# Loading a weight block's high part by a converting DMA and summing its low part from DRAM, in one stretch of a hybrid attention, RG-LRU and S5 block

## The chip, the cores and the metric

One core of a Trainium2 chip runs the program. The metric is device time in microseconds, the median of three runs: 1568.6 us before (1568.36, 1568.6 and 1571.8). One more execution was profiled; the rows shown further down are from it.

## The reference, cut to what matters

Two layers work on 512 latent and 256 context tokens of width 1024 (768 columns in all). One input projection feeds three mixers: differential attention, a bidirectional RG-LRU, and an S5 state space with a gated linear unit. Each mixer's output is multiplied by a SiLU gate, projected (`w_branch`), weighted by a sigmoid gate, and the sum goes through `w_out`. Everything is float32.

```
def hybrid_layer(x, ctx, c, c_ctx, p, layer_idx, need_ctx):
    ...
    q_l, k_l, v_l, za_l, xr_l, zr_l, us_l, zs_l, gl_l = jnp.split(h_l @ p['w_in'], pts, axis=-1)
    ...
    yr_l, yr_c = rglru_branch(xr_l, xr_c, p['conv_w'], p['conv_b'], p['lru_wa'], p['lru_ba'],
                              p['lru_wx'], p['lru_bx'], p['lru_lam'])
    ys_l, ys_c = s5_branch(us_l, us_c, p['s5_lam_re'], p['s5_lam_im'], p['s5_log_dt'], p['s5_b_re'],
                           p['s5_b_im'], p['s5_c_re'], p['s5_c_im'], p['s5_d'], p['s5_w_glu'],
                           p['s5_b_glu'], need_ctx)
    x = x + gt_x[:, None] * gated_merge(ya_l, yr_l, ys_l, za_l, zr_l, zs_l, gl_l, p['w_branch'], p['w_out'])

def gated_merge(ya, yr, ys, za, zr, zs, gl, w_branch, w_out):
    y = jnp.stack([ya * jax.nn.silu(za), yr * jax.nn.silu(zr), ys * jax.nn.silu(zs)], axis=2)
    yb = jnp.einsum('btnw,nwd->btnd', y, w_branch)
    g = jax.nn.sigmoid(gl.reshape(*gl.shape[:2], N_BRANCH, D_MODEL))
    return jnp.sum(g * yb, axis=2) @ w_out
```

## The kernel before

A float32 product is made of three products in the faster format fp32r: activations and weights are each split in a high part, rounded to fp32r, and a low part, the rest; high x high, low x high and high x low are summed (`product`, L169). Weights come in blocks of 128 x 512 float32 (256 KB). A block is four tiles of 128 x 128; each is used for three passes over 512 and 256 columns, 24 matmuls in all.

`wsplit` (L154) prepares a block. SyncE (SP) loads it into a buffer `wr`; ScalarE (ACT) writes the high part `wh` (L162); the low part `wl` is `wr - wh`. Mostly VectorE (DVE) subtracts (L167). Where `by_dma` is set, ACT writes `wl = -wh` (L164) and GpSimd (POOL) issues a DMA that adds `wr` to `wl` (L165), with the sum made by the DMA. `wr`, `wh` and `wl` have three buffers each in the pool `ws`; the gate weights of the RG-LRU (`wlru`) have one each in a pool of their own.

`by_dma` is set in the first layer only, from `lru` to the end of the merge of S5's output, for 56 blocks in this order: for each of four RG-LRU tiles the gate weights `wlru`, two blocks of in-projection (`inproj`) for the tile and two for each of two merge gates (`gate`), with S5 steps between them; eight for the four output gates of the RG-LRU (`merge_y`); eight of its branch projection (`branch`, called w1 to w8 below); four of S5's gated linear unit (`wglu`, g1 to g4); eight for S5's output gates (z1 to z8). Beside the last twelve, `s5_tables` computes tables for layer 1 on DVE and POOL stores them in DRAM (`s5d<-tb`, L401). Attention follows, with `by_dma` off.

A scheduler puts each engine's instructions in order ahead of time; each engine then goes through its own queue in that order, and an instruction that waits holds up all behind it. Buffers are used in turn: a block's `wh` and `wl` can be written when the matmuls on the block three before are done.

Of the kernel before, what the change touches and what calls it, by code (L numbers as in the profile page):

```python
# [11 lines left out]
F32 = mybir.dt.float32  # L12
F32R = mybir.dt.float32r
AF = mybir.ActivationFunctionType
OP = mybir.AluOpType
# [36 lines left out]
def hybrid_kernel(ctx, tc, xT, cc, wmod, win, winv, wbr, wout, wglu, wlru, par, lqk, s5a, s5b, s5B, s5C, dsk, rope, outT):  # L52
    nc = tc.nc
    V, S, G, PE, SP = nc.vector, nc.scalar, nc.gpsimd, nc.tensor, nc.sync
# [30 lines left out]
    def f32(ap):  # L85
        return ap.bitcast(F32)
# [65 lines left out]
    by_dma = [False]  # L152

    def wsplit(src, n, p=None, bufs=3, keep=None):  # L154
        p = p or pW
        raw = p.tile([128, 512], F32, name="wr", tag="wr", bufs=bufs)
        if keep:
            p, bufs = keep, None
        wh = p.tile([128, 512], F32R, name="wh", tag="wh", bufs=bufs)
        wl = p.tile([128, 512], F32R, name="wl", tag="wl", bufs=bufs)  # L160
        SP.dma_start(raw, src)
        S.activation(wh, raw, AF.Copy)  # L162
        if by_dma[0]:
            S.activation(wl, f32(wh), AF.Copy, scale=-1.0)  # L164
            G.dma_start(wl, raw, accum_op=OP.add)  # L165
        else:
            V.tensor_sub(wl, raw, f32(wh))  # L167
        return wh.rearrange("p (k n) -> p k n", n=n), wl.rearrange("p (k n) -> p k n", n=n)

# [548 lines left out]
    for l in range(L):  # L718
# [12 lines left out]
        def us_w(b, p):  # L731
            return [wsplit(win[l, US_T + i, :, 4 * b:4 * b + 4, :].rearrange("p k n -> p (k n)"), 128, keep=p)
                    for i in range(3)]
# [37 lines left out]
        def inproj(ct, sg, dst=None):  # L771
            blocks = []
            for b in range(2):
                wh, wl = wsplit(win[l, ct, :, 4 * b:4 * b + 4, :].rearrange("p k n -> p (k n)"), 128)
                blocks.append((wh, wl, 4 * b, 4))
            out = (dst or acc)("ps_in") if len(sg) > 1 else narrow("ps_in")
            product(blocks, hr, sg, out)
            return out
# [30 lines left out]

        def lru(i):  # L810
            wh, wl = wsplit(wlru[l, i].rearrange("p a n -> p (a n)"), 128, pR, 1)
            po = inproj(XR_T + i, both)
            xp = pR.tile([128, TT + 6], F32, name="xp", tag="up")
# [161 lines left out]
        for n in range(4):  # L975
            wh, wl = wsplit(wglu[l, n].rearrange("p k n -> p (k n)"), 128)
# [87 lines left out]
        for h in range(4):  # L1064
# [5 lines left out]
            for q0 in ([0, 2, 4] if need else [0, 2]):  # L1070
# [5 lines left out]
                for qi in range(2):  # L1076
                    qt = q0 + qi
                    p = [pT.tile([128, TT], F32, name=f"p{c}", tag=f"p{c}", bufs=2 - c) for c in range(2)]
# [20 lines left out]
                    for k0 in range(0, nk, 4):  # L1099
# [5 lines left out]
                        src = pt[:, :(k1 - k0) * 128].rearrange("p (k q) -> p k q", q=128)  # L1105
# [94 lines left out]
        for dt in range(KT):  # L1200
            late = dt >= KT - LATE
            blocks = []
            for b in range(2):
                wh, wl = wsplit(wout[l, dt, :, 4 * b:4 * b + 4, :].rearrange("p k n -> p (k n)"), 128,
                                keep=pK if late else None)
# [139 lines left out]
```

## Time and profile before

| | us |
|---|---|
| median of three runs | 1568.6 |
| the profiled execution | 1571.89 |
| its span, first to last instruction | 1570.1 |
| TensorE busy in it | 1489.2 |
| mean granted TensorE clock | 0.982 of full speed |

The profiled execution is 3.3 us above the median of the runs, and 1.8 us longer than its span. A stretch of the trace is named by the microseconds from the span's start.

### The profile page before, as it was taken

How to read it: one execution, taken by the hardware profiler on the slowest of the kernel's cores; microseconds unless marked ns; L12 is line 12 of the kernel's file. 1: busy time of each engine (PE TensorE's matmuls, PEld its weight loads, DVE VectorE, ACT ScalarE, POOL GpSimd, SP SyncE). 2: the span in 40 equal slices, each digit the busy share in tenths (PEclk: the TensorE clock that was granted, in tenths of full speed). 3: DMA queues.
4: the chain of work that ended last, by engine and by line, in shares of the span. 5: the costliest groups of instructions: out<-in, count | busy, mean ns of one | idle time of the engine just before them, and what ended most of it. 6: DMA issues, size and time to landing. Idle time of an engine off the chain costs nothing. (4 is left out here: it accounts for less than half of the span.)

```text
span 1570.1 us, 24750 instructions
## 1 busy us (share of the span) xinstructions
PE 1489.2 (95%) x9096; PEld 1246.2 (79%) x9096; DVE 1125.0 (72%) x2312; ACT 818.7 (52%) x1468; POOL 172.2 (11%) x231
## 2 busy tenths in 40 slices
PE   4998899899999999999999999999999999999997
PEld 2786778788988888888778887777788988888777
DVE  6789899978367757658568863789775488397555
ACT  6676878664344534534325365666525365355433
POOL 1111111124000100000332310000000000000110
PEclk8998999999999999989999999999999999999999
DMA  8555444467311111115573762435454212111542
GB/s 279 167 151 119 112 110 105 89 158 197 94 52 43 42 53 46 49 34 177 193 250 125 258 201 82 143 111 162 118 168 132 81 61 58 65 61 54 174 148 94
DMA packets 111210, 189.13 MB, mean 120 GB/s; under 512 B 25328, under 2 KB 42352, under 8 KB 111088
## 3 DMA queue, kind: packets, MB, share of 16 engines
q1 hardware_dynamic: 97392, 158.17, 32.2%
q0 software_dynamic: 13696, 29.37, 8.1%
q8 instruction: 72, 1.18, 0.3%
q14 instruction: 50, 0.41, 0.1%
HBM read 145.02 MB, written 25.69 MB: 109 GB/s over the span
## 5 line engine op out<-in xcount | busy, mean ns | idle before, releaser
L162 ACT ACTIVATE wh<-wr 128x512 fp32r<-128x512 f32 x320 | 200.3, 629 | 367.2 <-PE ps_in L180 151.3
L180 PE MATMUL ps_in<-hH,wh 128*128 128x512 f32 x1248 | 376.5, 360 | 14.4 <-ACT wh L162 7.3
L180 PE MATMUL ps_in<-hH,wl 128*128 128x512 f32 x1248 | 378.6, 359 | 7.1 <-DMA wl<-wr 7.1
L180 PE MATMUL ps_in<-hL,wh 128*128 128x512 f32 x1248 | 375.5, 359 | 0.0
L167 DVE TENSOR_TENSOR wl<-wr,wh 128x512 fp32r<-128x512 f32 x264 | 187.5, 714 | 172.7 <-ACT wh L162 129.9
L180 PEld LDWEIGHTS ps_in<-hH,wh 128*128 128x128 f32 x1248 | 207.3, 192 | 52.3 <-ACT wh L162 8.4
L180 PEld LDWEIGHTS ps_in<-hH,wl 128*128 128x128 f32 x1248 | 207.7, 191 | 43.1 <-DMA wl<-wr 9.6
L180 PEld LDWEIGHTS ps_in<-hL,wh 128*128 128x128 f32 x1248 | 206.9, 191 | 31.8
L911 POOL TENSOR_TENSOR m<-m,g 128x768 f32<-128x768 f32 (+1 forms) x16 | 29.0, 1811 | 730.7 <-issue 348.4
L1091 ACT ACTIVATE p<-ps_s,mx 128x768 f32<-128x768 f32 (+1 forms) x80 | 65.2, 815 | 71.4 <-DVE mx L1090 67.5
L180 PE MATMUL ps_b<-yH,wh 128*128 128x512 f32 (+1 forms) x288 | 89.5, 359 | 0.6 <-DVE m L945 0.6
L180 PE MATMUL ps_b<-yL,wh 128*128 128x512 f32 (+1 forms) x288 | 88.0, 357 | 0.0
L180 PE MATMUL ps_b<-yH,wl 128*128 128x512 f32 (+1 forms) x288 | 87.7, 357 | 0.0
L1089 DVE TENSOR_REDUCE mx<-ps_s 128x1 f32<-128x768 f32 (+1 forms) x80 | 67.6, 847 | 23.9 <-PE ps_s L1086 23.3
L165 POOL DMA_DIRECT2D wl<-wr x56 | 49.0, 896 | 259.6 <-ACT wl L164 206.1
L180 PEld LDWEIGHTS ps_b<-yH,wh 128*128 128x128 f32 x288 | 48.2, 188 | 10.7 <-ACT wl L164 0.9
L180 PEld LDWEIGHTS ps_b<-yL,wh 128*128 128x128 f32 x288 | 47.7, 188 | 7.2
L180 PEld LDWEIGHTS ps_b<-yH,wl 128*128 128x128 f32 x288 | 47.6, 188 | 7.2
L180 PE MATMUL acc<-mH,wh 128*128 128x512 f32 (+1 forms) x160 | 49.2, 340 | 0.0
L180 PE MATMUL acc<-mH,wl 128*128 128x512 f32 (+1 forms) x160 | 48.8, 337 | 0.0
L180 PE MATMUL acc<-mL,wh 128*128 128x512 f32 (+1 forms) x160 | 48.8, 337 | 0.0
L1107 DVE TENSOR_TENSOR wTL<-ps_t,wTH 128x512 fp32r<-128x512 f32 (+1 forms) x72 | 35.9, 536 | 13.4 <-ACT wTH L1106 13.2
(357 smaller groups left out, 2901.1 us busy)
## 6 DMA issues: line engine op xcount, KB each, us to landing
wr<-in_win SPq DMA_DIRECT2D x208, 256.0 KB
wm<-in_wmod SPq DMA_DIRECT2D x48, 512.0 KB
wl<-wr POOLq DMA_DIRECT2D x56, 256.0 KB, 3.9
wr<-in_wbr SPq DMA_DIRECT2D x48, 256.0 KB
sp<-s5d SPq DMA_DIRECT2D x16, 768.0 KB
wr<-in_wout SPq DMA_DIRECT2D x32, 256.0 KB
s5d<-vv POOLq DMA_DIRECT2D x16, 320.0 KB, 3.2
usd<-up SPq DMA_DIRECT2D x8, 512.0 KB
```

Of the source, the lines that this page charges most:

```text
L162: S.activation(wh, raw, AF.Copy)
L165: G.dma_start(wl, raw, accum_op=OP.add)
L167: V.tensor_sub(wl, raw, f32(wh))
L180: PE.matmul(out[:, c0:c0 + n], lhsT=(wl if ps == 2 else wh)[:, k, :], rhs=rhs(k0 + k, ps == 1)[:, t0:t0 + n], start=st, stop=en)
L911: (V if n == 0 and dt >= ADD_V[l] else G).tensor_add(m_t[dt][:, :W], m_t[dt][:, :W], g[:, :W])
L1089: V.reduce_max(mx[:, 0:1], sc[:, :kw], axis=AX.X)
L1091: S.activation(p[c][:, :kw], sc[:, :kw], AF.Exp, bias=mx[:, 1:2], scale=0.125, accum_out=sm[:, c:c + 1])
L1107: V.tensor_sub(wTL[:, k0:k1, qi * 128:(qi + 1) * 128], src, f32(wTH[:, k0:k1, qi * 128:(qi + 1) * 128]))
```

## The change

Where `by_dma` is set, the block is no longer loaded by SP. POOL issues a DMA from DRAM straight into `wh`, and that DMA converts float32 to fp32r. ACT writes `wl = -wh` as before, and POOL's second DMA adds the block to `wl` from DRAM, not from `wr`. `wr` is not used there. The other blocks are prepared as before.

```
     def wsplit(src, n, p=None, bufs=3, keep=None):
         p = p or pW
-        raw = p.tile([128, 512], F32, name="wr", tag="wr", bufs=bufs)
+        raw = None if by_dma[0] else p.tile([128, 512], F32, name="wr", tag="wr", bufs=bufs)
         if keep:
             p, bufs = keep, None
         wh = p.tile([128, 512], F32R, name="wh", tag="wh", bufs=bufs)
         wl = p.tile([128, 512], F32R, name="wl", tag="wl", bufs=bufs)
-        SP.dma_start(raw, src)
-        S.activation(wh, raw, AF.Copy)
         if by_dma[0]:
+            G.dma_start(wh, src)
             S.activation(wl, f32(wh), AF.Copy, scale=-1.0)
-            G.dma_start(wl, raw, accum_op=OP.add)
+            G.dma_start(wl, src, accum_op=OP.add)
         else:
+            SP.dma_start(raw, src)
+            S.activation(wh, raw, AF.Copy)
             V.tensor_sub(wl, raw, f32(wh))
```

Lines below L160 move by one at most (L162 and L164 are now the load and the accumulate, L163 the negation, L402 the store of the tables). The scheduler also makes a new order. On POOL, this is the queue of before, from the start of the stretch to the first stores of tables (`tb`):

```order
L165 DMA wl<-wr 128x512 x45
L401 DMA s5d<-tb 128x2x192 x4
L165 DMA wl<-wr 128x512 x2
L401 DMA s5d<-tb 128x2x192 x4
L165 DMA wl<-wr 128x512 x2
```

Nothing but accumulates stood in POOL's queue. Now each block has two entries. This is POOL's queue at the end of the first RG-LRU tile and the start of the second; the first two rows are the sixth block of `in_win`, the last one of the first tile's two gates, the rows behind them load `wlru` and the seventh to ninth block of `in_win`, with which the second tile begins:

```order
L162 DMA wh<-in_win 128x512
L164 DMA wl<-in_win 128x512
L162 DMA wh<-in_win 128x512
L162 DMA wh<-in_wlru 128x512
L162 DMA wh<-in_win 128x512 x2
L164 DMA wl<-in_wlru 128x512
L164 DMA wl<-in_win 128x512 x3
L162 DMA wh<-in_win 128x512
L164 DMA wl<-in_win 128x512
```

Load and accumulate alternate, but in the middle four loads stand together and the four accumulates behind them. And this is POOL's queue of now from the last branch projection (w8) through the gated linear unit to the first block of S5's output gates (z1):

```order
L162 DMA wh<-in_wbr 128x512
L164 DMA wl<-in_wbr 128x512
L162 DMA wh<-in_wglu 128x512
L402 DMA s5d<-tb 128x2x192 x4
L164 DMA wl<-in_wglu 128x512
L162 DMA wh<-in_wglu 128x512
L164 DMA wl<-in_wglu 128x512
L162 DMA wh<-in_wglu 128x512
L402 DMA s5d<-tb 128x2x192
L164 DMA wl<-in_wglu 128x512
L402 DMA s5d<-tb 128x2x192 x3
L162 DMA wh<-in_wglu 128x512
L162 DMA wh<-in_win 128x512
```

The alternation holds for w1 to g3; g4 and z1 are loaded together, and the stores of the tables stand between. After z1 it goes on in the same way: z2 to z4 alternate (with four stores of tables ahead of z2's accumulate, two ahead of z4's and two behind it), z5 with z6 and z7 with z8 are loaded in pairs.

On ACT, in the gated linear unit, the order of before was:

```order
L162 ACTIVATE wh<-wr 128x512
L164 ACTIVATE wl<-wh 128x512
L162 ACTIVATE wh<-wr 128x512
L981 ACTIVATE sg<-acc,prm 128x768
L164 ACTIVATE wl<-wh 128x512
```

and it is now:

```order
L163 ACTIVATE wl<-wh 128x512 x4
L982 ACTIVATE sg<-acc,prm 128x768 x2
L163 ACTIVATE wl<-wh 128x512 x2
L982 ACTIVATE sg<-acc,prm 128x768
L163 ACTIVATE wl<-wh 128x512
```

The conversions are gone, and the negations, each of which waits for a load, stand ahead of the gate's tanh (`sg`). On PE the matmuls of a block and their number stay; between 80 and 410 us rows of S5 and of the blocks change places by a few matmuls. From attention on, the order of all engines is that of before but for a few rows at its start.

## Rows read from the trace of the kernel before

**Rows 1.** The page: span, and busy us of each engine (share) xinstructions.

```profile
span 1570.1 us, 24750 instructions
...
PE 1489.2 (95%) x9096; PEld 1246.2 (79%) x9096; DVE 1125.0 (72%) x2312; ACT 818.7 (52%) x1468; POOL 172.2 (11%) x231
```

**Rows 2.** Windows: length, busy us of each engine, granted clock, DMA share, GB/s.

```profile
core 0: us, PE busy (x) PEld busy (x) DVE busy (x) ACT busy (x) POOL busy (x), PEclk, DMA share, GB/s
72.00:316.00 244.00, 222.04 (x1572) 184.80 (x1571) 223.11 (x475) 185.28 (x364) 31.90 (x37) 0.97 0.51 118
316.00:410.00 94.00, 90.36 (x530) 77.83 (x529) 67.15 (x184) 45.04 (x72) 27.59 (x34) 1.00 0.69 170
127.00:136.00 9.00, 4.80 (x13) 3.42 (x14) 9.00 (x24) 7.42 (x19) 2.60 (x3) 0.54 0.63 120
```

**Rows 3.** Waits from 72 to 410 us: us in total, times, longest.

```profile
POOL wl L165 <- ACT wl L164: 199.8, 35, 21.0
...
PE ps_in L180 <- ACT wh L162: 7.3, 3, 3.7
PE ps_in L180 <- DMA wl<-wr: 7.1, 6, 2.4
PE ps_y L663 <- DVE W L624: 4.5, 1, 4.5
PE ps_x L609 <- ACT ws L531: 2.6, 5, 0.8
```

**Rows 4.** Groups by line, 72 to 410 us: busy us, mean ns | idle before.

```profile
L162 ACT ACTIVATE wh<-wr 128x512 fp32r<-128x512 f32 x59 | 36.6, 625 | 48.3 <-PE ps_in L180 19.0 <-PE ps_b L180 11.2 <-DMA wr<-in_win 9.7
```

**Rows 5.** DMA issues of the page: KB each, median us from issue to landing.

```profile
wl<-wr POOLq DMA_DIRECT2D x56, 256.0 KB, 3.9
...
s5d<-vv POOLq DMA_DIRECT2D x16, 320.0 KB, 3.2
...
s5d<-ws POOLq DMA_DIRECT2D x16, 256.0 KB, 3.3
...
s5d<-tb POOLq DMA_DIRECT2D x16, 192.0 KB, 3.4
```

**Rows 6.** Tiles wl (whole span; 180 to 192 us) and tb: ns, landing us min/median/max.

```profile
L165 POOL DMA_DIRECT2D wl<-wr x56: 847/859/1210, 67.0 to 398.5; - x56
...
DMA to landing us min/median/max: 3.2/3.9/6.7
...
DMA to landing us min/median/max: 3.2/4.5/4.9
...
L401 POOL DMA_DIRECT2D s5d<-tb x16: 707/747/989, 351.1 to 388.5; - x16
...
DMA to landing us min/median/max: 2.5/3.4/4.4
```

**Rows 7.** Timeline of ACT and POOL, 118 to 135 us: start, us, instruction.

```profile
118.08 1.58 ACT L853 ACTIVATE th<-th,tiny 128x1536 f32<-128x1536 f32 x1
...
122.58 0.62 ACT L164 ACTIVATE wl<-wh 128x512 fp32r<-128x512 f32 x1
...
126.73 1.14 ACT L162 ACTIVATE wh<-wr 128x512 fp32r<-128x512 f32 x2
...
123.50 0.86 POOL L165 DMA_DIRECT2D wl<-wr  x1 [21.04 <-ACT wl L164]
```

**Rows 8.** Timeline of PE, 122 to 142 us.

```profile
122.81 0.88 PE L609 MATMUL ps_x<-vt,ws 128*64 128x96 f32 x16
127.40 0.69 PE L180 MATMUL ps_in<-hH,wh 128*128 128x512 f32 x2 [3.71 <-ACT wh L162]
...
131.97 1.01 PE L180 MATMUL ps_in<-hH,wh 128*128 128x512 f32 x2 [3.23 <-ACT wh L162]
...
134.19 1.01 PE L180 MATMUL ps_in<-hH,wl 128*128 128x512 f32 x2 [0.57 <-DMA wl<-wr]
```

**Rows 9.** Timeline of PE: first three blocks and what follows; first and last of 316-410.

```profile
81.44 0.62 PE L180 MATMUL ps_in<-hH,wh 128*128 128x512 f32 x2
...
94.79 0.88 PE L609 MATMUL ps_x<-vt,ws 128*64 128x96 f32 x16
...
316.46 0.39 PE L180 MATMUL ps_b<-yH,wh 128*128 128x512 f32 x1
...
409.80 0.64 PE L1014 MATMUL ps_v<-wh,hH 128*128 128x256 f32 x4
```

**Rows 10.** Waits of SP's queue, 72 to 410 us.

```profile
SPq L161 <- DMA wl<-wr: 131.5, 37, 8.7
SPq L673 <- ACT yo L670: 29.7, 10, 7.0
```

More of the change, by code (lines that the diff above doesn't have):

```diff
@@ L155, in wsplit @@
         p = p or pW
-        raw = p.tile([128, 512], F32, name="wr", tag="wr", bufs=bufs)
+        raw = None if by_dma[0] else p.tile([128, 512], F32, name="wr", tag="wr", bufs=bufs)
         if keep:
@@ L160, in wsplit @@
         wl = p.tile([128, 512], F32R, name="wl", tag="wl", bufs=bufs)
-        SP.dma_start(raw, src)
-        S.activation(wh, raw, AF.Copy)
         if by_dma[0]:
+            G.dma_start(wh, src)
             S.activation(wl, f32(wh), AF.Copy, scale=-1.0)
-            G.dma_start(wl, raw, accum_op=OP.add)
+            G.dma_start(wl, src, accum_op=OP.add)
         else:
+            SP.dma_start(raw, src)
+            S.activation(wh, raw, AF.Copy)
             V.tensor_sub(wl, raw, f32(wh))
```

## The prediction

> **What bounds the kernel now.** I began with the busy times of the page [rows 1]: TensorE (PE) works 1489.2 of 1570.1 us, ScalarE (ACT) 818.7 and GpSimd (POOL) 172.2, so only time in which PE stands still can be won. The change touches 56 weight blocks, all between 72 and 410 us but for the first POOL transfer, so I cut that stretch in two with a table of windows [rows 2]. From 72 to 316 us (RG-LRU, S5 scans, merge of the RG-LRU output; 36 blocks) PE is busy 222.0 of 244 us, VectorE (DVE) 223.1 and ACT 185.3: three engines nearly full. From 316 to 410 us (RG-LRU's branch projection, the gated linear unit, the merge of its output; 20 blocks w1 to w8, g1 to g4, z1 to z8) PE is busy 90.4 of 94 us and the others are not. Idle PE is thus 22.0 + 3.6 us, and the granted clock of 0.97 in the first part costs 0.03 x 244 = 7 us: 33 us is all that can be won. The waits [rows 3] say for what PE waits there: for a high part that ACT writes late 7.3 us, for a low part that lands late 7.1 us, for S5 4.5 and 2.6 us. The same view shows POOL waiting 199.8 us for ACT's negation: it has time to spare, but always in front of a wait.
>
> **What is removed.** 56 conversions on ACT at 625 ns [rows 4], 35 us of an engine that is not the bound; only where PE waits for them do they count. The worst such place is shown by three rows of PE [rows 8]: 3.71 + 3.23 + 0.57 = 7.5 us of waits between 123.7 and 134.2 us, because the conversions stand in ACT's queue behind other work until 126.73 us [rows 7]. The granted clock is 0.54 from 127 to 136 us [rows 2], so mostly the lower of its two levels (1.2 of 2.4 GHz), after PE had stood still: about (1 - 0.54) x 9 = 4 us more. 56 loads also leave SP's queue, which waits 131.5 us for buffers of these blocks [rows 10], with S5's transfers behind them.
>
> **What is added.** POOL gets 56 more issues at 0.86 us [rows 6], 48 us busy beside 172.2; as a sum this is nothing. What counts is order. A block's high part and low part share POOL's queue as load, accumulate, load, accumulate, and the accumulate waits until the load has landed and ACT has negated it. The next load waits behind it. One round of POOL is: load from issue to landing, L; one hop to ACT; ACT's queue; negation 0.62; one hop to POOL; accumulate's issue 0.86. A hop is 0.3: the negation that began at 122.58 and took 0.62 is followed by POOL's issue at 123.50 [rows 7]; the same is taken for the hop from a landing. ACT's queue: between nothing and its longest operation there, 1.58 [rows 7]; I take 0.2, since its mean operation from 316 to 410 us is 45.04 / 72 = 0.63 us and it is busy 48% of the time [rows 2], and half an operation is left on average.
>
> L has no row, since no load of weights on POOL's queue exists. The nearest are POOL's own transfers: landing in 3.4, 3.3 and 3.2 us for the three stores of 192 to 320 KB and 3.9 for the accumulate of 256 KB [rows 5]; one store took 2.5, and in a stretch with the accumulates crowded the median was 4.5 [rows 6]. Ends: 2.5 and 4.5. I take 3.4, the stores, since only the accumulate reads its destination too. The round is then 3.4 + 0.3 + 0.2 + 0.62 + 0.3 + 0.86 = 5.7 us (4.8 at L = 2.5, 6.8 at L = 4.5).
>
> One page of the Trainium skill speaks of L: "DMA: Bandwidth & Descriptors", section "Anatomy of one DMA - SWDGE (gpsimd) path", gives 2.0 us + bytes / 436e3 for such a transfer, 2.6 us for 262,144 bytes. The accumulate's row is above it (3.9); for a plain load no row decides, and by the page's figure the round is 4.9 us and the sum below comes out at nothing. That is the first rival.
>
> **316 to 410 us.** PE goes through 20 blocks from 316.46 to 409.80 us [rows 9], 4.67 us a block. Until z4 POOL's new order has alternating rounds with one pair (loads of g4 and z1, then both accumulates: 0.86 more than a round for two blocks). From the load of w1 to that of z5 that is 14 x 5.7 + 6.6 = 86.4 us. S5 table stores of 0.75 us [rows 6] stand between: those ahead of an accumulate fit into its wait (four take 3.0, load to accumulate is 4.8 us); those behind one add 5 x 0.75 = 3.7. Together 90.1 us, against 16 x 4.67 = 74.7 on PE: 15.4 late. POOL starts with a lead: a low part is ready 4.8 + 3.9 = 8.7 us after its load's issue, and the three buffers let the load go two blocks and 0.7 us (the two wh products that come first) ahead of need; at 4.67 us a block that is 10.0 us, at 244 / 36 = 6.8 us (the pace before 316) 14.3. Lead between 1.3 and 5.6; I take 3.5. So **+12 us** (0 at L = 2.5; 28 at 4.5: each 0.1 us of the round is 1.5 us here). The accumulate from DRAM in place of SBUF is taken at 3.9 us too; it lies behind POOL's round, and moves only the lead, by as much as it differs (3.2 to 4.5).
>
> **72 to 316 us.** At 6.8 us a block POOL's 5.7 keeps up on average, not in bursts. At the start three blocks follow each other on PE at 4.4 us (81.44 to 94.79 us [rows 9]): about 1 us late for two of them, +2. Where the second RG-LRU tile begins, the loads of blocks 7 to 9 stand ahead of all their accumulates (the second fence of the section on the change). The load of block 9 waits for its buffer until PE is done with block 6, the one just before block 7, and behind it comes the accumulate of the gate weights; so block 7's low part, which PE needs at once, lands 2 x 0.86 + 3.9 = 5.6 us later, and PE stands 5.6 - 0.7 = 4.9 us and loses some 3 us by the clock: 8 in place of the 7.5 + 4 that this place costs before, -3. Beyond that ACT's negation now waits for landings with S5's and RG-LRU's evacuations queued behind it; three engines are nearly full, so I put +3 for it, between nothing and 8 places (four RG-LRU tiles, four merges) of 2.5 us, 20. In sum **+2** for this part; its ends are -11 (the 7.3 us of late high parts and 4 of clock vanish and nothing comes) and +20.
>
> The tail from 410 us on keeps its order and its time. Sum: +14 us on the profiled execution's 1571.9, 1586 us; the median of the runs before is 1568.6, 3.3 below that execution, so **1583 us**. A difference of 0.2%, 3 us, is what a measurement here can tell from no change.
>
> **Rivals.** *POOL keeps up.* With L below about 2.8 the round is below 5.1 and 316 to 410 us loses 2 us at most; -3 to +3 in all, 1566 to 1572 us. For it: loads end in SBUF, the stores in DRAM, and nothing is read back. Against it: 3.2 us is the fastest accumulate, which also ends in SBUF.
> *Faster.* L as short, and the first part's place at 123 us goes with ACT's 35 us; 7.3 of high parts, 3.5 (half) of late low parts and 4 of clock: -8 to -15, 1554 to 1561 us. It decides where L is under 2.8 and ACT, not POOL, is late; for it speaks ACT's late conversion at 126.73, against it that the negation stays in ACT's queue, and that the loads had been prefetched by SP into buffers of their own, three blocks ahead, while they now wait for the buffer that PE frees.
> *Much slower.* L at 4.5 or ACT's queue at 1 us: +28 in the second part, +15 to +20 in the first, and stalls of 4 us that halve the clock after each, as at 127 us: +40 to +70, 1609 to 1639 us. For it: DMA engines are 0.69 busy from 316 us on [rows 2].
> That the change does not do what it says can be left out: the order shows 56 loads on POOL and no conversion on ACT.
>
> **Chances.** Forecast (+4 to +35 us) 0.57, POOL keeps up 0.16, faster 0.13, much slower 0.14. Faster by over 0.2%: 0.13 and a quarter of the second case, 0.17; within: 0.11; slower 0.72. The range runs from 1561 (leaving out part of the faster case) to 1622 us (leaving out half of the much slower one).
>
> **What would show it.** Right: from 316 us POOL's issues in rounds of 5.5 to 6 us with hardly an idle buffer, PE waiting for low parts of nearly each w and z block, and the second part 10 to 15 us longer; L between 3 and 4; SP's 131.5 us of waits gone; ACT's busy time 35 us less. Wrong: L under 2.8 or over 4.2; a first part that shrinks by more than 3 us; POOL waiting for PE's buffers rather than for ACT; a changed time after the last z block.

## The result, and the profile after

The changed kernel takes 1617.7 us (median of four runs, 1614.34 to 1621.57) beside 1570.2 us before on the same chip: a ratio of 1.0301, interval 1.0276 to 1.0326. The forecast was 1583 us. The direction is right and the time lies in the range of 1561 to 1622 us, but the loss is 47 us in place of 14, beyond the +4 to +35 us that were the forecast proper.

The page of after, with the rows that answer to [rows 1] and [rows 5] (for the loads and accumulates of `in_win`: times, KB, median us from issue to landing):

```profile
span 1617.8 us, 24627 instructions
...
PE 1499.4 (93%) x9096; PEld 1254.2 (78%) x9096; DVE 1124.4 (70%) x2312; ACT 788.3 (49%) x1412; POOL 200.5 (12%) x287
...
wh<-in_win POOLq DMA_DIRECT2D x40, 256.0 KB, 4.4
wl<-in_win POOLq DMA_DIRECT2D x40, 256.0 KB, 4.3
```

ACT is 30.4 us less busy than before, POOL 28.3 us more, as the edits say; PE does the same 9096 matmuls in a span that is 47.7 us longer. The load lands after 4.4 us, where the forecast took 3.4.

Where the time went is read from two matmuls on PE's timeline, the first of the RG-LRU's branch projection (`ps_b`) and the first of attention (`ps_v`); before, they stood at 316.46 and 409.80 us [rows 9]. After:

```profile
339.72 0.60 PE L181 MATMUL ps_b<-yH,wh 128*128 128x512 f32 x2
...
459.25 0.64 PE L1015 MATMUL ps_v<-wh,hH 128*128 128x256 f32 x4
```

So the first part (up to `ps_b`) is **23.3 us** longer, where the forecast had 2, and the second (from there to `ps_v`) is 119.5 in place of 93.3 us, **26.2 us** longer, where it had 12. The rest takes 1617.8 - 459.25 = 1158.5 us, 1.8 less than before. The windows of the two parts, and of two stretches that follow stalls of PE in the first:

```profile
core 0: us, PE busy (x) PEld busy (x) DVE busy (x) ACT busy (x) POOL busy (x), PEclk, DMA share, GB/s
72.00:339.70 267.70, 228.17 (x1576) 190.49 (x1575) 221.80 (x474) 165.64 (x325) 51.67 (x74) 0.93 0.50 107
339.70:459.20 119.50, 96.46 (x523) 80.54 (x522) 67.14 (x183) 34.36 (x54) 37.23 (x52) 0.96 0.59 134
103.00:112.00 9.00, 6.93 (x34) 5.23 (x35) 8.76 (x18) 4.06 (x9) 2.29 (x3) 0.62 0.39 79
223.00:232.00 9.00, 7.85 (x44) 7.15 (x45) 7.14 (x17) 3.10 (x6) 1.40 (x2) 0.62 0.31 58
```

The granted clock is 0.93 and 0.96, where it was 0.97 and 1.00 [rows 2]: in each of the two short stretches the clock is mostly at the lower of its two levels for some microseconds, 0.38 x 9 = 3.4 us, behind stalls of 1.6 to 3.4 us. Stalls are paid a second time there. In all, PE's idle time from 72 us to `ps_v` grows from 22.0 + 3.6 us [rows 2] to 39.5 + 23.0, and its busy time by 12 us with the same matmuls, part of them at the lower clock: together the 49 us that the two parts lost.

The waits of the whole stretch, 72 to 459 us (us in total, times, longest):

```profile
POOL wl L164 <- ACT wl L163: 180.8, 44, 8.1
POOL wh L162 <- PE ps_in L181: 71.0, 21, 13.4
ACT wl L163 <- DMA wh<-in_win: 66.9, 24, 6.0
...
PE ps_in L181 <- DMA wl<-in_win: 13.6, 8, 3.5
...
PE ps_in L181 <- DVE sz L874: 11.4, 1, 11.4
...
PE acc L181 <- DMA wl<-in_wglu: 8.1, 3, 4.3
...
PE ps_b L181 <- DMA wl<-in_wbr: 7.6, 4, 2.9
PE ps_x L610 <- ACT ws L532: 7.1, 8, 3.4
```

PE's waits for low parts are 29 us, where they were 7.1 [rows 3]; 19.6 of them (8.1, 7.6 and 3.9) lie in the second part, where 1.9 lay before. The waits for high parts are gone. POOL still spends most of its idle time on ACT's negation, and ACT now waits for landings itself. PE's longest wait, 11.4 us for DVE's `sz` at the end of the first part (0.4 us before), is not a loss by itself: the run with four buffers below has it too, at 10.9 us, and reaches `ps_b` only 2 us late. But it shows that PE is not alone on the path there: in the first part DVE has the same work (221.8 us) and stands still for 46 us in place of 21. Which of DVE's waits reach `ps_b` was not followed.

The rounds of POOL in the second part, from its timeline (start, us, instruction, in brackets the idle time before it):

```profile
369.96 0.85 POOL L164 DMA_DIRECT2D wl<-in_wbr  x1 [8.11 <-ACT wl L163]
370.50 0.87 POOL L162 DMA_DIRECT2D wh<-in_wbr  x1
376.22 0.85 POOL L164 DMA_DIRECT2D wl<-in_wbr  x1 [4.84 <-ACT wl L163]
376.76 0.87 POOL L162 DMA_DIRECT2D wh<-in_wbr  x1
382.27 0.84 POOL L164 DMA_DIRECT2D wl<-in_wbr  x1 [4.64 <-ACT wl L163]
```

They have the form of the forecast: the load 0.54 us behind the accumulate's start, then a wait for landing and negation. These two rounds take 6.26 and 6.05 us. How long a load needs to land depends on what stands ahead of it. The last row of the view of tile wh, for 72 to 110 us, 115 to 150 us and 345 to 450 us in this order:

```profile
DMA to landing us min/median/max: 4.4/5.4/6.1
DMA to landing us min/median/max: 2.7/3.0/3.8
DMA to landing us min/median/max: 2.9/4.8/8.0
```

In the first stretch every load, and in the third 8 of 17, is issued within 1 us behind an accumulate; from 115 to 150 us none of the five loads has an accumulate within 4 us ahead of it. Load by load, over the whole kernel, the median of the loads that come next behind an accumulate is 4.8 us for the 22 that follow it by under 1 us (the fastest lands in 4.1), 4.7 for 8 that follow by 1 to 2 us, 3.1 for 5 at 2 to 4 us and 3.1 for 8 at 4 us or more. It need not be an accumulate: two loads 0.5 to 0.6 us behind another load, and two 0.7 us behind a store of tables, land in 4.8 to 5.0 us, although the last accumulate was issued 2.0 to 3.3 us before them. The Trainium skill, "DMA: Bandwidth & Descriptors", section "Anatomy of one DMA - SWDGE (gpsimd) path", gives 2.0 us + bytes / 436e3, an estimate of 2.6 us for this size; the trace comes near that (2.7 to 3.0 for four of the five loads from 115 to 150 us, 3.8 for the fifth) only for loads with nothing just ahead of them.

### The profile page after: what moved, and what is told of

Read it like the earlier page. It is cut to its first block, busy times and chain, and to the rows that moved or that the text cites. A ratio compares the mean times of both kernels' runs of the same rounds, so it can differ in the third digit from the quotient of the medians.

```text
span 1617.8 us, 24627 instructions
## 1 busy us (share of the span) xinstructions
PE 1499.4 (93%) x9096; PEld 1254.2 (78%) x9096; DVE 1124.4 (70%) x2312; ACT 788.3 (49%) x1412; POOL 200.5 (12%) x287
## 3 DMA queue, kind: packets, MB, share of 16 engines
q1 hardware_dynamic: 89328, 143.48, 28.3%
## 5 line engine op out<-in xcount | busy, mean ns | idle before, releaser
L167 ACT ACTIVATE wh<-wr 128x512 fp32r<-128x512 f32 x264 | 165.5, 630 | 323.9 <-PE ps_in L181 134.5
L163 ACT ACTIVATE wl<-wh 128x512 fp32r<-128x512 f32 x56 | 35.0, 629 | 117.5 <-DMA wh<-in_win 66.9
L181 PEld LDWEIGHTS ps_b<-yH,wh 128*128 128x128 f32 x288 | 48.3, 190 | 11.4 <-ACT yH L879 1.7
L164 POOL DMA_DIRECT2D wl<-in_win x40 | 35.3, 883 | 143.3 <-ACT wl L163 123.7
```

The source lines that it names most:

```text
L164: G.dma_start(wl, src, accum_op=OP.add)
L181: PE.matmul(out[:, c0:c0 + n], lhsT=(wl if ps == 2 else wh)[:, k, :], rhs=rhs(k0 + k, ps == 1)[:, t0:t0 + n], start=st, stop=en)
```

## The experiments

The change and the four rows below it stood beside 1570.2 us of before; "four buffers, alternating", "three buffers, load ahead", "low from SBUF" and "before with four buffers" beside 1571.63; "late issue" and "negation on POOL" beside 1567.36; "four buffers, load ahead" and "second part alone" beside 1568.57; the last one beside 1573.3. "First part" is the start of `ps_b` (316.5 us before), "second part" the time from there to `ps_v` (93.3), both from the profile; "rest" is what follows (1160.3).

| run | first part | second part | rest | median | ratio, interval |
|---|---|---|---|---|---|
| the change | 339.7 | 119.5 | 1158.5 | 1617.7 | 1.0301 (1.0276 to 1.0326) |
| low half alone | 326.0 | 98.4 | 1162.2 | 1587.25 | 1.0107 (1.0081 to 1.0134) |
| high half alone | 336.6 | 119.0 | 1156.6 | 1616.85 | 1.0299 (1.0272 to 1.0326) |
| raw loads by POOL | 318.5 | 101.4 | 1161.0 | 1582.45 | 1.0082 (1.0059 to 1.0106) |
| four buffers | 318.5 | 96.2 | 1165.9 | 1582.24 | 1.0079 (1.0049 to 1.0108) |
| four buffers, alternating | 356.2 | 119.2 | 1163.3 | 1642.16 | 1.045 (1.0412 to 1.0489) |
| three buffers, load ahead | 324.5 | 108.5 | 1158.1 | 1592.02 | 1.0135 (1.0111 to 1.016) |
| four buffers, load ahead | 322.3 | 94.8 | 1168.4 | 1585.07 | 1.0102 (1.0086 to 1.0119) |
| four buffers, low from SBUF | 315.5 | 99.3 | 1171.3 | 1593.34 | 1.0155 (1.0118 to 1.0192) |
| before with four buffers | 315.4 | 95.5 | 1167.9 | 1582.31 | 1.0075 (1.0048 to 1.0102) |
| late issue | 389.1 | 136.7 | 1172.4 | 1698.94 | 1.0821 (1.0784 to 1.0859) |
| negation on POOL | 361.4 | 143.0 | 1164.6 | 1663.26 | 1.0587 (1.0549 to 1.0625) |
| second part alone | 314.2 | 119.7 | 1156.1 | 1601.36 | 1.0203 (1.0186 to 1.022) |
| ACT free of landings | 331.4 | 121.4 | 1166.2 | 1616.62 | 1.026 (1.0237 to 1.0283) |

**Which half costs it.** Low half alone, against before: SP loads and ACT converts, only the accumulate reads DRAM.

```diff
-            G.dma_start(wl, raw, accum_op=OP.add)
+            G.dma_start(wl, src, accum_op=OP.add)
```

> The low half of the change alone: SyncE still loads wr and ScalarE still converts it to wh, but the accumulate reads the block from DRAM. Theory A (POOL's round: a load waits in POOL's queue behind the accumulate of the block before, which waits for its own load to land and be negated) has no load on POOL here: 1565 to 1574 us, within 0.3% of before, with the accumulate landing in 3.9 to 4.4 us. Theory B (the accumulate from DRAM is what is slow): at least 20 us slower than before, 1588 us or more.

It gave 17 us, between the two theories. The accumulate lands in 4.9 us (median) in place of 3.9 and PE waits 17.1 us for low parts from 72 us to `ps_v`, where it was 7.1; the scheduler's order on PE changed too, so these 17 us are not put down to the landing alone.

High half alone, against the change: POOL loads and converts, SP loads `wr` as well, and the accumulate reads that.

```diff
-        raw = None if by_dma[0] else p.tile([128, 512], F32, name="wr", tag="wr", bufs=bufs)
+        raw = p.tile([128, 512], F32, name="wr", tag="wr", bufs=bufs)
...
+        SP.dma_start(raw, src)
...
-            G.dma_start(wl, src, accum_op=OP.add)
+            G.dma_start(wl, raw, accum_op=OP.add)
```

> The high half of the change alone: POOL's converting load writes wh, SyncE loads wr as well (one more load of each block), and the accumulate reads wr. Theory A: all of the loss is here, 1605 to 1630 us. Theory B: 1568 to 1580 us. The 256 KB more of each block on the DMA engines may add a few us by either.

The same time as the whole change, in both parts: the loads on POOL's queue are enough for all of the loss. The halves by themselves lose 17 and 47 us, more than the whole, so the two losses do not add up.

**The conversion, or the queue.** Against before, POOL issues the load of `wr`, without conversion; `wr` has its own three buffers, and the order puts most loads ahead of the accumulate of the block before.

```diff
-        SP.dma_start(raw, src)
+        (G if by_dma[0] else SP).dma_start(raw, src)
```

> The kernel before, but POOL and not SyncE loads wr (no conversion, three buffers of its own, so the order puts a load or two ahead of the accumulate before it). Theory A: the round is not closed any more, since the load does not wait for a buffer that TensorE frees last: 1568 to 1588 us. Theory C (it is the conversion in the DMA that is slow): the load lands in 3.2 to 3.5 us here, against 4.4 of the converting one, and the time is within 5 us of before; without C it lands in 4.0 to 4.6 us here too.

The loss is 12 us. The issues of the page for `in_win`, of this run and of the next one, whose loads convert:

```profile
wr<-in_win POOLq DMA_DIRECT2D x40, 256.0 KB, 3.4
```

```profile
wh<-in_win POOLq DMA_DIRECT2D x40, 256.0 KB, 3.7
```

Over all 56 loads the medians are 3.2 and 3.7 us. But the next run has nine loads within 1 us behind an accumulate, and this run has one. In like places, 4 us or more behind an accumulate, it is 3.0 us without conversion (21 loads) and 3.1 with it (18). So the landing is the one that theory C named, but by the place in the queue and not by the conversion, of which hardly a price is left to see; the total is theory A's.

**Order or buffers.** Against the change, four buffers for the high parts (`wlru`'s `wr` is gone, which leaves the room); with them the scheduler puts most loads ahead of the accumulate of the block before.

```diff
-        wh = p.tile([128, 512], F32R, name="wh", tag="wh", bufs=bufs)
+        wh = p.tile([128, 512], F32R, name="wh", tag="wh", bufs=4 if bufs == 3 else bufs)
```

> The changed kernel with four buffers for wh in place of three. The order then has one load ahead of the accumulate of the block before for most blocks, so two blocks share a landing. Theory A: a block costs POOL's queue two issues and one wait for what landed long before, so most of the loss goes: 1572 to 1592 us. Theory C: landing and accumulate follow each other as before, and a fourth buffer gives at most a third of the loss back: 1600 to 1615 us.

35 of the 47 us come back. But this edit changed order and buffers at once. Three more runs fill the table of the two: four buffers with each load queued behind the last accumulate, three with each load ahead of it, four with each load ahead.

```diff
+            if by_dma[1:]:
+                with tc.issue_after(by_dma.pop().ins):
+                    G.dma_start(wh, src)
...
-            G.dma_start(wl, src, accum_op=OP.add)
+            by_dma.append(G.dma_start(wl, src, accum_op=OP.add))
```

> The change with four buffers for the high parts, but POOL's queue is made to alternate: every load stands behind the accumulate of the block before, everywhere. Theory A, the order in POOL's queue costs the time: the round stays load, negation, accumulate, some 6.0 to 6.7 us for landings of 3.7 to 4.4 us, and 316 to 410 us lasts 15 to 27 us longer than before, whatever the buffers; the run is at 1598 to 1620 us. Theory B, it was the wait for the buffer that PE frees: with a fourth buffer the load never waits for PE, and the run is at 1578 to 1592 us like the change with four buffers.

```diff
-            G.dma_start(wh, src)
+            ld = G.dma_start(wh, src)
...
+            if by_dma[1:]:
+                tc.add_manual_dep(by_dma.pop().ins, ld.ins.name, mybir.DependencyInfo(mybir.DependencyClass.NoSync, mybir.DependencyReason.DATA), reason="load first")
+            by_dma.append(G.dma_start(wl, src, accum_op=OP.add))
```

> The change with three buffers as it is, but every load is made to stand ahead of the accumulate of the block before. Theory A, the order costs the time: 30 to 40 us come back, 1576 to 1592 us. Theory B, the buffers cost it: the load waits for the matmuls three blocks before, the accumulate is now queued behind this wait, and lands after PE needs it; 1610 us or more.

The same edit with four buffers:

> Four buffers for the high parts, and every load is made to stand ahead of the accumulate of the block before: the fourth of the four cases of order and buffers. Theory A, both what the queue's order is and how long a load waits for the matmuls' buffer count: it is the fastest of the four, 1572 to 1586 us, and POOL's waits for the matmuls' buffers, 230 us with three, fall by half. Theory B, the order alone counts: as with three buffers, 1588 to 1596 us.

With the load ahead it is 1592.0 and 1585.1 us with three and four buffers; alternating everywhere with four buffers it is 1642.2, more than the change, which has three but does not alternate at each place. The order decides with either number of buffers (theory A of the first two), though both sizes were off: 1642 us lies above the first range, and with three buffers 26 us came back where 30 to 40 were expected. The second part shows how the two work together: it lasts 119.5 us (the change, three buffers) and 119.2 (four) where loads alternate with accumulates, 108.5 and 94.8 with the load ahead. So the order alone gives 11 of the 26 us back, and the fourth buffer 14 more, but only where the load is ahead; alternating, it gives nothing. In the medians these 14 us shrink to 7 (5 by the ratios, each beside its own runs of before), since the rest is 10 us longer with four buffers (more on this below). POOL's waits for the buffers that PE frees fall by a quarter, from 225 to 170 us, not by half. POOL's waits, first alternating with four buffers, then ahead with three, then ahead with four:

```profile
POOL wl L168 <- ACT wl L167: 239.5, 50, 10.1
...
POOL wh L164 <- PE ps_g L185: 28.1, 3, 15.9
```

```profile
POOL wh L162 <- PE ps_in L183: 184.7, 38, 13.2
...
POOL wh L162 <- PE ps_b L183: 23.8, 6, 6.9
POOL wl L166 <- ACT wl L163: 23.1, 12, 4.5
```

```profile
POOL wh L162 <- PE ps_in L183: 135.3, 30, 15.0
POOL wl L166 <- ACT wl L163: 66.3, 38, 4.8
```

Alternating with four buffers, POOL waits for PE's buffers in few places (28.1 us in three), so mostly a buffer is free and nobody loads it: POOL stands at an accumulate. With the load ahead the wait is mostly for PE, which means that POOL is early. The landing shows the same in these three (tile wh, last row of the view: alternating, ahead with three, ahead with four it is 4.4, 3.2 and 3.4 us in the median).

**What makes the landing long.** Against the run that alternates with four buffers: small additions on POOL between accumulate and load.

```diff
                 with tc.issue_after(by_dma.pop().ins):
+                    for _ in range(4):
+                        sp = G.tensor_scalar(pad, pad, 1.0, None, op0=OP.add)
+                with tc.issue_after(sp.ins):
                     G.dma_start(wh, src)
```

> The run with four buffers and forced alternation (1642 us; a load is issued 0.55 us behind the accumulate before it and lands 4.4 us later in the median) with four small additions of some 0.42 us on POOL between every accumulate and the next load, so that the load is issued some 1.7 us later. Theory A, a load's landing is long because its packets queue behind those of the accumulate ahead of it: the load then lands 2.9 to 3.3 us after its issue, POOL's round grows by 0.5 us at most, and the run is at 1640 to 1665 us. Theory B, 4.4 us is what a load takes in this stretch, whatever stands ahead of it: the landing stays at 4.2 to 4.6 us, the round grows by 1.7 us, and the run is at 1670 us or more.

One round of POOL's timeline, and the landing of the loads (tile wh):

```profile
383.56 0.88 POOL L173 DMA_DIRECT2D wl<-in_wbr  x1 [3.65 <-ACT wl L172]
384.15 1.50 POOL L167 TENSOR_SCALAR pad<-pad 128x8 f32<-128x8 f32 x4
385.63 0.58 POOL L169 DMA_DIRECT2D wh<-in_wbr  x1
391.00 0.87 POOL L173 DMA_DIRECT2D wl<-in_wbr  x1 [4.79 <-ACT wl L172]
```

```profile
DMA to landing us min/median/max: 2.9/3.3/5.4
```

The loads land in 3.3 us in place of 4.4: a load's landing is long because of the accumulate just ahead of it on the queue, as theory A has it, and 4.4 us is not what a load takes here. The total is theory B's, and the round grows by 0.9 us, between the two: the load now starts 2.9 us (median) behind the accumulate in place of 0.56, 2.3 later, and gets back only 1.1 of it; the second part has 136.7 / 20 = 6.8 us a block in place of 6.0. Which piece of the path makes the load wait behind the accumulate (its descriptors or its packets) no row says.

**The second part by itself.** The 36 blocks of the first part as before, the 20 of the second as the change; against the change, in part:

```diff
...
-        if by_dma[0]:
+        if by_dma[0] == 2:
             G.dma_start(wh, src)
...
-            V.tensor_sub(wl, raw, f32(wh))
+            if by_dma[0]:
+                S.activation(wl, f32(wh), AF.Copy, scale=-1.0)
+                G.dma_start(wl, raw, accum_op=OP.add)
+            else:
+                V.tensor_sub(wl, raw, f32(wh))
...
+        by_dma[0] = 2 * (l == 0)
         for dt in range(KT):
             s5_go(PLAN[l][5][dt])
```

> The change only in the second part: from the RG-LRU's branch projection on (20 blocks) the blocks are prepared as the change does, with three buffers and POOL's queue alternating; the 36 blocks ahead of it are prepared as before. Theory A, the two parts lose apart, each by its own order: the first part ends at 314 to 319 us, the second is 17 to 28 us longer than before (a round with loads that land in 4.4 us), 1586 to 1599 us. Theory B, the forecast's own size for the second part, with loads that land in 3.4 us: 12 us longer, 1578 to 1585 us. Theory C, the second part is slow only since the first hands it no lead in POOL's queue: 5 us longer at most, 1569 to 1577 us.

```profile
314.19 0.39 PE L185 MATMUL ps_b<-yH,wh 128*128 128x512 f32 x1
...
433.93 0.52 PE L1020 MATMUL ps_v<-wh,hH 128*128 128x256 f32 x3
```

The first part is back and the second lasts 119.7 us, 26.4 more than before: theory A. The second part loses its time without any help from the first; the first with the change alone was not run. The median of the runs, 1601.4, is above its range; the profiled execution took 1591.8, and what sets the executions of this kernel 8 to 11 us apart was not looked into.

**The first part: POOL or ACT.** Negation on POOL in place of ACT:

```diff
-            S.activation(wl, f32(wh), AF.Copy, scale=-1.0)
+            G.tensor_scalar(wl, f32(wh), -1.0, None, op0=OP.mult)
```

> The change with the negation on POOL in place of ACT, so that ACT's queue holds nothing of these blocks; POOL still waits for each landing. Theory A, in the first part the loss comes from ACT's negations, which wait for landings with S5's and the RG-LRU's evacuations behind them: PE's waits for ACT (ws, st, strip, gi) there go, the first branch projection starts at 316 to 328 us in place of 340, and the run is at 1590 to 1608 us. Theory B, the loss comes from POOL's round alone, which keeps its length within 0.5 us: the first branch projection starts at 335 us or later, and the run is at 1612 to 1630 us.

It doesn't tell: the negation takes 1.98 us on POOL (mean of 56; the median is 1.70) in place of 0.63 on ACT, so POOL's round grew and both parts with it, and 1663 us lies beyond both ranges. So another run kept POOL's wait and took ACT's away (`zero` is a column of zeros that is set at the start):

```diff
-            S.activation(wl, f32(wh), AF.Copy, scale=-1.0)
+            S.activation(wl, zero.to_broadcast([128, 512]), AF.Copy, scale=-1.0)
+            G.tensor_scalar(wl[:, :1], f32(wh[:, :1]), -1.0, None, op0=OP.mult)
             G.dma_start(wl, src, accum_op=OP.add)
```

> The change with ACT's queue freed of waits for landings: ACT writes wl from a constant zero, which is ready, and a POOL operation on one column of wh stands in front of the accumulate, so that POOL still waits for each load before it issues the accumulate. wl then holds the block less its first column, not the low part: this part of the computation is changed. POOL's queue keeps nearly the order of the change, and its round loses the negation of 0.62 us and gains an operation of some 0.42 us. Theory A, the 23 us of the first part come from S5's and the RG-LRU's evacuations that stand behind ACT's negations: PE's waits for ACT there fall under 6 us in all, and the first branch projection starts at 316 to 328 us. Theory B, they come from POOL's round, whose low parts are late: it starts at 333 to 345 us. By both the second part stays 18 to 28 us longer than before.

PE's waits in the first part, of the change and then of this run:

```profile
PE ps_in L181 <- DMA wl<-in_win: 9.7, 5, 3.5
PE ps_x L610 <- ACT ws L532: 6.5, 7, 3.4
PE ps_y L666 <- ACT st L655: 4.7, 4, 2.9
PE ps_wt L530 <- ACT strip L499: 2.5, 3, 1.6
PE ps_g L181 <- ACT gi L841: 2.2, 2, 1.7
PE ps_in L181 <- ACT up L791: 1.4, 2, 1.2
```

```profile
PE ps_in L184 <- DMA wl<-in_win: 20.6, 8, 5.6
PE ps_x L613 <- ACT ws L535: 2.5, 5, 0.9
PE ps_wt L533 <- ACT strip L502: 0.7, 1, 0.7
```

The waits for ACT fall from 17.3 us (the last five rows of the first) to 4.3 (the last two of the second, and three more of 0.3 to 0.4), and `ps_b` comes at 331.4 us, between the two ranges: 8 of the 23 us come back. The two causes overlap, since PE's waits for low parts double, from 9.7 to 20.6 us, when those for ACT go. So 8 us is what ACT's waits for landings cost with POOL's round nearly as it is, and this run does not show that the other 15 are POOL's round alone. What does bear on it are the runs with loads ahead of accumulates: there the first part ends at 318.5 to 324.5 us, so 15 to 21 of the 23 us go with the order of the queue. The second part is as long as with the change, as both theories had it. The total hardly falls, since the rest takes 8 us longer in the profiled execution.

**Is there a faster version?** The high half alone (above) with four buffers, so that the accumulate reads SBUF as before:

```diff
-        raw = p.tile([128, 512], F32, name="wr", tag="wr", bufs=bufs)
+        raw = pW.tile([128, 512], F32, name="wr", tag="wr", bufs=3) if bufs == 1 else p.tile([128, 512], F32, name="wr", tag="wr", bufs=bufs)
...
-        wh = p.tile([128, 512], F32R, name="wh", tag="wh", bufs=bufs)
+        wh = p.tile([128, 512], F32R, name="wh", tag="wh", bufs=4 if bufs == 3 else bufs)
```

> The change with four buffers for the high parts, and the accumulate reads SBUF as before: SP loads the block a second time into wr (the gate weights' wr in the pool of the others). It tells what the 12 us are that the four buffers left. Theory A, the accumulate from DRAM costs them, which lands 0.6 to 0.9 us later: 1568 to 1576 us. Theory B, they come from loads in POOL's queue and from ACT's negations that wait for landings: 1579 to 1588 us.

The kernel before with the same two edits:

> The kernel before with four buffers for the high parts (the gate weights' wr in the pool of the others). It tells whether the fourth buffer is worth something by itself. Theory A, it is not: 1566 to 1574 us, and what it gave in the changed kernel came from the order that it allows. Theory B, it is, since PE's waits for late high parts, 7.3 us and the lower clock behind them, go: 1555 to 1565 us.

Neither is, and the first lies above both of its ranges. Both reach attention within 5 us of before (414.7 and 410.9 us in place of 409.8) and lose 11 and 8 us behind it, where the change does nothing: the fourth buffer holds for the later blocks too, and the scheduler makes another order there. The run with four buffers also loses 5.6 of its 12 us in the rest. In the table the rest takes 1163.3 to 1172.4 us in the six kernels with four buffers (mean 1168.2) and 1156.1 to 1166.2 in the nine with three, before included (mean 1160.4), and those nine all have the same order on PE there. So some 8 us go with the fourth buffer, but a single pair of runs can differ by as much without it. Up to `ps_v` the source of the accumulate explains none of those 12 us (theory A of the first falls), and the fourth buffer is worth nothing by itself (theory A of the second, though its range was too low). No version tried beats the kernel before.

## Why the prediction was right in direction and wrong in size

The forecast was short by 33 us: 14 in the second part, 21 in the first, and 2 came back in the rest.

- **What bounds, what is removed.** Right in that ACT is not the bound: its busy time fell by 30.4 us and the kernel is slower. SP's waits for these buffers [rows 10] are gone, and SP waits for S5's output `yo` from ACT instead (98.5 us in place of 29.7). The high parts that came late [rows 8] no longer do.
- **POOL's round as the mechanism of the second part.** Right: load, accumulate, load, accumulate, with PE waiting for low parts, though in 10 places and not at nearly each block. Undoing only this order gives 26 of the 47 us back, with a fourth buffer 33, and the 20 blocks alone lose 26 us.
- **L = 3.4 us, the step that failed.** The forecast took L from the stores, "since only the accumulate reads its destination too". Measured is 4.4 over all, just inside the upper end of 4.5 that it had kept, and 4.8 from 345 to 450 us, beyond it. All but two of the stores that it took the price from were issued 3 us or more behind the last accumulate; here the load is issued 0.54 us behind an accumulate on the same queue, and takes 4.8 us there but 3.1 with 4 us between. The forecast had drawn this order and then priced the load without its neighbour. With 4.4 its own formula gives 14 x 6.7 + 7.6 + 3.7 - 74.7 - 3.5 = 27 us, and 26.2 were measured (from the load of w1 at 325.63 to that of z5 at 432.58 us: 107 us, formula 105). So near an agreement is in part luck. From landing to negation 0.02 to 0.10 us pass for each of these 17 loads, where the forecast had 0.5, and the next load starts 0.54 us behind the accumulate and not 0.86, so a round with a landing of 4.5 us takes 6.05 and not 6.8. What makes up for it is not in the formula: 7.2 us in which POOL waits for PE's buffers, and a load (at 360.98 us) that lands in 8.0.
- **The lead** of 3.5 us and the accumulate at 3.9 (4.3 measured) were not told apart from this. The source of the accumulate made no difference beside loads by POOL (second part 119.5 and 119.0 with three buffers, 96.2 and 99.3 with four); why the low half alone, with the accumulate as the only thing changed, loses 17 us stays open.
- **The first part, +2 forecast, +23 measured.** The terms that failed are the +3 for ACT's queue and the late low parts, which it counted at the start (+2) and at the second tile, and put at nothing elsewhere. By the first `ps_g` of each RG-LRU tile the delay is 8.8, 7.3, 19.3 and 20.8 us. The burst at the start cost 8.8 in place of 2: the loads there land in 5.4 us, the same error as above, and the lower clock from 103 us on is a part of it. The second tile's place gained 1.5 of the 3 forecast: PE's wait there was 3.46 us, with 4.9 forecast. The third tile lost 12 us, with two stalls behind ACT's queue of 2.94 and 3.43 us; the clock is 0.62 behind the second (223 to 232 us). This is the second:

```profile
222.85 0.63 ACT L163 ACTIVATE wl<-wh 128x512 fp32r<-128x512 f32 x1 [1.96 <-DMA wh<-in_win]
223.50 0.60 ACT L532 ACTIVATE ws<-ps_wt 128x512 f32<-128x512 f32 x1
...
224.15 1.55 PE L610 MATMUL ps_x<-vt,ws 128*64 128x96 f32 x16 [3.43 <-ACT ws L532]
```

  ACT's negation waits for the landing, the evacuation `ws` stands behind it, and PE behind that. This was forecast as +3 and its end as 20. PE's waits for ACT there are 17.3 us, where evacuations cost it 4.3 before; without them 8 us come back, and late low parts take the place of the others. The forecast had these at the start and at the second tile alone: "at 6.8 us a block POOL's 5.7 keeps up on average" was worked out with the short L, and with 6.1 to 6.7 little slack is left. That a shorter landing with the same order would have saved the first part is argued, not shown: no run has it.
- **The rival that came near** is the much slower one (L at 4.5; 1609 to 1639 us, given 0.14). It had the right place and nearly the right price, and the halved clock behind stalls; its +28 and +15 to +20 are the measured 26 and 23 within a few microseconds.
- **Behind 410 us** nothing changed, as forecast (-1.8 us).

## What to carry to other kernels

A DMA queue that carries a load, then an accumulate that depends on it, then the next load, runs at the sum of the whole chain: price one round of it, and put the next load ahead of the dependent transfer, with a buffer free for it: here the order gave 11 us of the second part's 26 back, the fourth buffer in that order 14 more. Take a transfer's landing from a row with the same neighbours on its queue, not from the nearest transfer of its size; where both ends of a range are far apart and the sum is 16 rounds, the choice between them is the forecast. A fast engine's short instruction that waits for a landing holds all behind it: count the queue behind it, not its own 0.6 us.

## What was not expected of the hardware

- The same load lands in 3.0 us (median of five, 2.7 to 3.8) with nothing just ahead of it and in 4.8 (up to 8.0) when issued within 1 us behind an accumulate on POOL's queue; four small additions between the two take the median of the alternating run from 4.4 back to 3.3. Behind another load or a store it is 4.8 to 5.0 too (four loads).
- The conversion from float32 to fp32r in the load has no price that shows: 3.1 us with it and 3.0 without, for loads 4 us or more behind an accumulate.
- A load's issue begins 0.54 us behind the start of an accumulate whose own row says 0.85 us: the forecast counted 0.86 on the path, 0.3 too much.
- Negating 128 x 512 elements takes 1.98 us in the mean on POOL (median 1.70), 0.63 on ACT.
- A buffer more for one kind of tile goes with some 8 us more in the rest of the kernel, where neither its blocks nor its work changed but the scheduler's order did; how much of it is the order and how much the scatter between runs (10 us with the same order) is not shown.
